# Hybrid decoder trunk on one core: six places for split weights, earlier index scores, and a later scale and shift of the residual rows

## The chip, the cores and the metric

The kernel runs on 1 core of a Trainium2 chip. The metric is device microseconds (us) of one execution, and the median of several is compared. Engines are named as the profile names them: PE (TensorE matmuls), PEld (TensorE weight loads), DVE (VectorE), ACT (ScalarE), POOL (GpSimd) and SP (SyncE, which issues most DMAs).

## The reference

One decoder layer on 512 tokens of width 1024, everything in float32. Each of three sub-layers is applied as h <- LayerNorm(ALPHA * h + f(h)).

1. Token mixing. One input projection feeds three groups of heads: gated linear attention (GLA, 4 heads), sparse attention (DSA, 5 heads) and stick-breaking attention (SB, 5 heads). The outputs are concatenated and go through `w_out`.
2. Cross-attention with 4 heads into 256 memory tokens (`w_mem_q`, `w_mem_kv`, `w_mem_o`).
3. A squared-ReLU MLP of hidden width 4096 (`w_up`, `w_down`).

The sparse attention picks its keys by an index score:

```python
rel = relu(einsum('bthd,bsd->bths', iq, ik))         # 8 index heads of 64
isc = einsum('bths,bth->bts', rel, iw) * idx_scale   # weighted sum over the heads
isc = where(causal, isc, -inf)
_, idx = top_k(isc, 128)                             # keys that query t may see
```

## The kernel before

All matmuls of projections take fp32r operands in two parts, a rounded high part and the rest. A weight tile of 128x1024 is loaded by a DMA into one of 4 places (`wr_pool`), `split` (L419) writes the high part to one of 5 places in `wh_pool` and the low part to one of 5 in `wl_pool` (L383, L384), and `mm3` (L414) makes three matmuls of each pair. Other tiles lie in 31 pages of 4 KB per partition (`page`, L392), 8 half-size places of 2 KB (`temp`, L395), 8 PSUM banks, and in constants of their own (`cst`). The constants `scan_mask`, `rel`, `cmask_f`, `cmask`, `tri_f`, `ones_f` and `w2p` are such.

The stages come in this order: LayerNorm of the input and its transposes; the index projection `ik` and four tiles `iq` of two heads each; GLA value, query and key projections (`gv_glr`, three `gqk_tile`, L674); index scores and top-k; GLA; SB; DSA with the keys and values of the memory between; `w_out` with a norm (`after_mix`, L1147); the four memory heads; `w_mem_o` with a norm (`after_mem`, L1198); the MLP, whose up part interleaves with seven-product down part (`first_products`, L1271; `second_parts`, L1319).

A matmul group that gets `split=True` (L590) makes its 512 columns in two halves of 256, so that it can start when only the first half of the tokens is normed. Of the `iq` tiles, heads 0, 2 and 4 are split so.

For each block j = 1 to 3 of 128 queries the index scores take eight heads of two matmuls, a Relu on ACT and a multiply-add on DVE into `acc` (128 x 128(j+1)). `top_k(j)` (L712) then makes 16 rounds of `max` and `match_replace` on DVE, and at the end writes the mask `E[j]`, which only DSA reads (L1038).

**What sets the order.** No instruction is issued when the Python code reaches it. `Program.either` (L163) records it with a priority, the running counter `nc.clock`, which grows by one per instruction. At the end `Program.issue` (L240) lays all of them out by a list scheduler: each engine takes the ready instruction that can start first, and among equals the one with the lowest priority number; an instruction is only looked at when its number is at most `LOOK` = 560 ahead of the first one not yet issued, and a tile is only handed out early when its pool has a place left for all that comes before it (`slots`, L275). Each engine then runs its list in that order. So a change of a priority or of a pool's size can reorder every engine's list.

A piece of code can move its instructions in that order by changing the counter. Top-k does so, one round every `TOPK_STRETCH` = 10 instructions:

```python
start = nc.clock
for n, _ in enumerate(s for j in range(1, NT) for s in top_k(j)):
    nc.clock = start + (n + 1) * TOPK_STRETCH
nc.clock = start
```

and so does the scale and shift of the residual rows, which are normed in place (`center`, L518) and whose gain and bias are needed only when the row is next added to:

```python
def gain_shift(hat, gb, t, later=0.0):
    nc.clock += later
    any_tt(hat[t], hat[t], gb[0], OP.mult)
    any_tt(hat[t], hat[t], gb[1], OP.add)
    nc.clock -= later
```

`any_tt` (L407) offers an instruction to DVE first and to POOL second. Behind `w_out` and behind `w_mem_o` four rows of 128x1024 each get a multiplication and an addition, `GAIN_LATER` = 400 instructions behind (L1155, L1209); their rows of gain and bias take two pages till then.

Of the kernel before, what the change touches and what calls it, by code (L numbers as in the profile page):

```python
# [364 lines left out]
def trunk_kernel(ctx: ExitStack, tc: tile.TileContext, x, mem, ln_in_g, ln_in_b, w_in, gate_w2,  # L365
# [17 lines left out]
    wh_pool = pool("wh", "wh", 5)  # L383
    wl_pool = pool("wl", "wl", 5)  # L384
# [58 lines left out]
    scan_mask = cst.tile([128, 512], F32, "scan_mask")  # L443
# [125 lines left out]
    rel = cst.tile([128, 512], F32, "rel")  # L569
    nc.gpsimd.iota(rel, pattern=[[1, 512]], base=-384, channel_multiplier=-1, allow_small_or_imprecise_dtypes=True)  # L570
    cmask_f = cst.tile([128, 128], F32, "cmask_f")
    nc.gpsimd.memset(cmask_f, 1.0)
    nc.gpsimd.affine_select(out=cmask_f, in_=cmask_f, pattern=[[1, 128]], compare_op=OP.is_ge, fill=0.0,
                            base=0, channel_multiplier=-1)
    nc.gpsimd.memset(cmask_f[0:64, 64:128], 0.0)
    cmask = cst.tile([128, 128], U32, "cmask")
    nc.vector.tensor_copy(cmask, cmask_f)
    tri_f = cst.tile([128, 128], F32, "tri_f")
# [5 lines left out]
    ones_f = cst.tile([128, 128], F32, "ones_f")  # L584
# [106 lines left out]
    E_pg = [page([1024], F32, "E012"), page([512], F32, "E3")]  # L691
    E = [E_pg[0][:, 0:128], E_pg[0][:, 128:384], E_pg[0][:, 384:768], E_pg[1][:, 0:512]]
    accs = {}
    for j in range(1, NT):
        n = 128 * (j + 1)
        acc = temp(f"acc{j}")
        accs[j] = acc
        for h in range(IDX_H):
            ps = bank("ps_idx")
            for i in range(2):  # L700
                mm(ps[:, :n], iq[h][:, 128 * j:128 * j + 128], ik[:, i, 0:n], i == 0, i == 1)
            r = temp("r")
            nc.scalar.activation(r[:, :n], ps[:, :n], AF.Relu)
            if h == 0:
                nc.vector.tensor_scalar(acc[:, :n], r[:, :n], iw[:, j, 0:1], None, op0=OP.mult)
            else:
                nc.vector.scalar_tensor_tensor(acc[:, :n], r[:, :n], iw[:, j, h:h + 1], acc[:, :n],
                                               op0=OP.mult, op1=OP.add)
        nc.gpsimd.affine_select(out=acc[:, n - 128:n], in_=acc[:, n - 128:n], pattern=[[-1, 128]],
                                compare_op=OP.is_ge, fill=MASKED, base=0, channel_multiplier=1)  # L710

    def top_k(j):  # L712

        n = 128 * (j + 1)
        acc = accs[j]
        for _ in range(TOPK // 8):
            m8 = tiny(8, "m8")
            nc.vector.max(m8, acc[:, :n])
            nc.vector.match_replace(out=acc[:, :n], in_to_replace=m8, in_values=acc[:, :n], imm_value=TAKEN)
            yield  # L720
# [11 lines left out]
    w2p = cst.tile([16, 2, 2, 64], F32, "w2p")  # L732
# [34 lines left out]
    for i in range(1, 3):  # L767
        gqk_tile(i)
# [648 lines left out]
```

## Time and profile before

| what | value |
|---|---|
| median of 3 runs | 826.19 us (826.02 to 827.07) |
| the profiled execution | 825.4 us, of which the span from the first to the last instruction is 823.6 us |
| PE busy | 792.5 us (96% of the span), 4177 matmuls |
| PEld busy | 662.8 us (80%) |
| DVE busy | 631.3 us (77%) |
| ACT busy | 329.2 us (40%) |
| POOL busy | 158.2 us (19%) |
| DMA | 106.70 MB, mean 130 GB/s |

Busy time is the union of an engine's instructions. A matmul's end is modelled, so a busy PE can still be short of its best pace; start times of neighbouring matmuls show the pace. An idle stretch of an engine is put down to the instruction that released it last. Times in the rows count from the span's start.

### The profile page before, as it was taken

The numbers are of one execution on the slowest core, as the hardware profiler recorded it, in microseconds if no ns is written. First come the engines' busy times: TensorE is split into PE (matmuls) and PEld (weight loads), VectorE is DVE, ScalarE is ACT, GpSimd is POOL, SyncE is SP. The second block draws the span as 40 slices with busy tenths as digits, with TensorE's granted clock in tenths as the row PEclk, the third lists the DMA queues.
The fourth block names the chain that finished last, engine by engine and source line by source line (L and its number), as shares of the span: only waits on it lengthen the run. The fifth ranks groups of instructions, "written<-read, shape, count | busy, mean of one in ns | idle before, by whom it ended". The sixth has DMA issues, their size and how long they took to land.

```text
span 823.6 us, 11289 instructions
## 1 busy us (share of the span) xinstructions
PE 792.5 (96%) x4177; PEld 662.8 (80%) x4177; DVE 631.3 (77%) x1111; ACT 329.2 (40%) x634; POOL 158.2 (19%) x173
## 2 busy tenths in 40 slices
PE   7999999999999899989999989999999999899995
PEld 5997769777877888888878889888888888678884
DVE  7737999997649983886553799767777776798778
ACT  4506634577535540233330143333323232585420
POOL 5320142354622210227340210000000000110001
PEclk9999999999999999999999999999999999999998
DMA  8520331603244534023322024645546555467532
GB/s 239 137 53 15 100 94 27 179 9 103 75 152 159 165 120 150 27 77 103 114 92 77 26 77 142 217 154 186 197 137 214 196 174 175 138 219 240 196 126 103
DMA packets 99927, 106.70 MB, mean 130 GB/s; under 512 B 10448, under 2 KB 79136, under 8 KB 99872
## 3 DMA queue, kind: packets, MB, share of 16 engines
q1 hardware_dynamic: 97344, 99.00, 38.1%
q10 hardware_dynamic: 2528, 6.98, 2.5%
q8 instruction: 33, 0.54, 0.3%
q14 instruction: 22, 0.18, 0.1%
HBM read 94.69 MB, written 10.49 MB: 128 GB/s over the span
## 4 chain that ended last, share of the span: by engine, by line
PE 68%; DVE 16%; issue 2%; ACT 1%; DMA 1%; POOL 0%; DVEq 0%; ACTq 0%; POOLq 0%
PE ps_up L356 20%; PE ps_dn L356 17%; PE ps_wmo L356 4%; PE ps_wo L356 4%; PE ps_q L356 3%; DVE res L356 2%; PE ps_km L356 2%; PE ps_z L356 2%; DVE acc L356 2%; PE ps_vm L356 2%; PE ps_gg L356 1%; PE ps_dq L356 1%; PE ps_mo L356 1%; DVE m L356 1%; DVE s L356 1%
## 5 line engine op out<-in xcount | busy, mean ns | idle before, releaser
L356 PE MATMUL ps_up<-h2T,h_up 128*128 128x512 f32 (+1 forms) x576 | 161.1, 366 | 0.0
L356 PEld LDWEIGHTS ps_up<-h2T,h_up 128*128 128x128 f32 x576 | 104.0, 189 | 17.6 <-DVE h2T L356 0.2
L356 PE MATMUL ps_up<-h2T,l_up 128*128 128x512 f32 (+1 forms) x288 | 104.8, 366 | 0.5 <-DVE l_up L356 0.5
L356 ACT ACTIVATE ur<-ps_up,gb_all 128x512 f32<-128x512 f32 x32 | 22.1, 690 | 108.7 <-PE ps_up L356 108.7
L356 PEld LDWEIGHTS ps_up<-h2T,l_up 128*128 128x128 f32 x288 | 54.1, 189 | 9.5 <-DVE l_up L356 0.7
L356 PE MATMUL ps_dn<-h_dn,a 128*128 128x512 f32 x192 | 59.3, 389 | 0.0
L356 DVE TENSOR_TENSOR l_dn<-r_dn,h_dn 128x1024 fp32r<-128x1024 f32 (+1 forms) x44 | 45.2, 1026 | 5.1 <-ACT h_dn L356 3.7
L356 PE MATMUL ps_dn<-h_dn,ends 128*128 128x512 f32 x128 | 47.7, 396 | 0.7 <-DVE ends L356 0.7
L356 POOL TENSOR_TENSOR a<-keep,a 128x1024 fp32r<-128x1024 f32 x1 | 4.1, 4067 | 228.3 <-PE ps_dn L356 228.3
L356 PE MATMUL ps_q<-h1T,h_wmq 128*128 128x256 f32 (+1 forms) x192 | 45.7, 329 | 0.0
L356 ACT ACTIVATE h<-ps_lt,gb_all 128x256 f32<-128x256 f32 x20 | 10.2, 566 | 85.6 <-PE ps_lt L356 84.8
L356 PEld LDWEIGHTS ps_dn<-h_dn,a 128*128 128x128 f32 x192 | 36.0, 188 | 7.5
L356 PE MATMUL ps_wmo<-h_wmo,oT 128*128 128x512 f32 x128 | 40.7, 393 | 0.0
L356 DVE TENSOR_TENSOR l_up<-r_up,h_up 128x1024 fp32r<-128x1024 f32 x32 | 38.9, 1220 | 2.2 <-ACT h_up L356 0.5
L356 PE MATMUL ps_wo<-h_wo,mix 128*128 128x512 f32 x128 | 40.3, 392 | 0.0
L356 PE MATMUL ps_dn<-l_dn,a 128*128 128x512 f32 x96 | 37.3, 389 | 0.0
L356 PEld LDWEIGHTS ps_q<-h1T,h_wmq 128*128 128x128 f32 x192 | 32.9, 197 | 2.5 <-DVE h1T L356 0.2
L356 PE MATMUL ps_q<-h1T,l_wmq 128*128 128x256 f32 (+1 forms) x96 | 31.3, 330 | 0.5 <-DVE ve_mix L356 0.5
L356 DVE TENSOR_SCALAR h_up<-r_up 128x1024 fp32r<-128x1024 f32 x17 | 11.8, 692 | 26.1 <-PE ps_up L356 22.6
L356 PEld LDWEIGHTS ps_dn<-h_dn,ends 128*128 128x128 f32 x128 | 24.5, 192 | 6.3 <-DVE ends L356 1.2
L356 PEld LDWEIGHTS ps_wo<-h_wo,mix 128*128 128x128 f32 x128 | 24.0, 188 | 4.9
L356 PEld LDWEIGHTS ps_wmo<-h_wmo,oT 128*128 128x128 f32 x128 | 24.0, 188 | 4.8
(408 smaller groups left out, 2095.6 us busy)
## 6 DMA issues: line engine op xcount, KB each, us to landing
r_dn<-in_w_down_dram SPq DMA_DIRECT2D x48, 512.0 KB, 4.3
r_up<-in_w_up_dram SPq DMA_DIRECT2D x32, 512.0 KB, 4.5
r_t<-t SPq DMA_DIRECT2D x16, 512.0 KB, 3.6
r_kvv<-in_w_mem_kv_dram SPq DMA_DIRECT2D x8, 512.0 KB, 4.0
r_kvk<-in_w_mem_kv_dram SPq DMA_DIRECT2D x8, 512.0 KB, 3.6
r_wo<-in_w_out_dram SPq DMA_DIRECT2D x8, 512.0 KB, 4.4
r_wmq<-in_w_mem_q_dram SPq DMA_DIRECT2D x8, 512.0 KB, 5.0
r_wmo<-in_w_mem_o_dram SPq DMA_DIRECT2D x8, 512.0 KB, 3.4
```

The costliest lines, as they stand in the source:

```text
L356: f(*[real(a) for a in args], **{k: real(a) for k, a in kwargs.items()})
```

## The change

It does three things.

First, `wh_pool` and `wl_pool` get 6 places each instead of 5. The room comes from the constants: `scan_mask` and `rel` share one page (`masks`), and `cmask_f`, `cmask`, `tri_f`, `ones_f` and `w2p` become half-size places that are handed on when their last reader is done. `cmask` is made just ahead of GLA. In `first_weights` the order in which the two pairs of places are asked for changes, not their number.

Second, the index scores of a pair of heads are recorded right behind the `iq` tile of the next pair, and those of the last pair at the head of `top_k(j)`; top-k starts right behind the last tile, ahead of `gv_glr`, one round every 18 instructions instead of 10. The third `iq` tile is no longer split in halves. The first `gqk_tile`, which was recorded ahead of the index scores, now follows with the other two behind the decay terms.

Third, `GAIN_LATER` is 900 instead of 400.

```diff
-    wh_pool = pool("wh", "wh", 5)
-    wl_pool = pool("wl", "wl", 5)
+    wh_pool = pool("wh", "wh", 6)
+    wl_pool = pool("wl", "wl", 6)
...
-    scan_mask = cst.tile([128, 512], F32, "scan_mask")
+    masks = page([2, 512], F32, "masks")
+    scan_mask, rel = masks[:, 0, :], masks[:, 1, :]
...
-    rel = cst.tile([128, 512], F32, "rel")
...
-    tri_f = cst.tile([128, 128], F32, "tri_f")
+    tri_f = temp("tri_f", 128)
...
-    ones_f = cst.tile([128, 128], F32, "ones_f")
+    ones_f = temp("ones_f", 128)
...
-    iq = new_q("iq", IDX_H)
-    for h in range(0, IDX_H, 2):
-        ps = proj_T([(C_IQ + 64 * h, 128, 0)], "iq", split=h < 6, weights=second if h == 0 else None)
-        for e in range(2):
-            stack(iq[h + e], ps, 64 * e, 1.0)
...
+    iq = new_q("iq", IDX_H)
+    accs = {j: temp(f"acc{j}") for j in range(1, NT)}
+
+    def index_scores(h, j):
+
+        n, acc = 128 * (j + 1), accs[j]
+        ps = bank("ps_idx")
+        for i in range(2):
+            mm(ps[:, :n], iq[h][:, 128 * j:128 * j + 128], ik[:, i, 0:n], i == 0, i == 1)
+        r = temp("r")
+        nc.scalar.activation(r[:, :n], ps[:, :n], AF.Relu)
+        if h == 0:
+            nc.vector.tensor_scalar(acc[:, :n], r[:, :n], iw[:, j, 0:1], None, op0=OP.mult)
+        else:
+            nc.vector.scalar_tensor_tensor(acc[:, :n], r[:, :n], iw[:, j, h:h + 1], acc[:, :n],
+                                           op0=OP.mult, op1=OP.add)
+
+    def iq_tile(h):
+        ps = proj_T([(C_IQ + 64 * h, 128, 0)], "iq", split=h < 4, weights=second if h == 0 else None)
+        for e in range(2):
+            stack(iq[h + e], ps, 64 * e, 1.0)
+
+    for h in range(0, IDX_H, 2):
+        iq_tile(h)
+        if h:
+            for j in range(1, NT):
+                for e in range(2):
+                    index_scores(h - 2 + e, j)
...
+        for e in range(2):
+            index_scores(IDX_H - 2 + e, j)
+        nc.gpsimd.affine_select(out=acc[:, n - 128:n], in_=acc[:, n - 128:n], pattern=[[-1, 128]],
+                                compare_op=OP.is_ge, fill=MASKED, base=0, channel_multiplier=1)
...
-    start, nc.pace = nc.clock, GQK_PACE
-    gqk_tile(0)
-    nc.clock, nc.pace = start, 1.0
...
-    w2p = cst.tile([16, 2, 2, 64], F32, "w2p")
+    w2p = temp("w2p", 256)[0:16].reshape(2, 2, 64)
...
+    cmask_f = temp("cmask_f", 128)
...
+    cmask = temp("cmask", 128, U32)
+    nc.vector.tensor_copy(cmask, cmask_f)
...
-    for i in range(1, 3):
+    for i in range(3):
         gqk_tile(i)
...
-        hi = [wh_pool.tile([128, n], F32R, f"h_dn{n}") for n in (512, 1024)]
-        lo = [wl_pool.tile([128, n], F32R, f"l_dn{n}") for n in (512, 1024)]
+        left = [wh_pool.tile([128, 512], F32R, "h_dnl"), wl_pool.tile([128, 512], F32R, "l_dnl")]
+        hi, lo = wh_pool.tile([128, 1024], F32R, "h_dn"), wl_pool.tile([128, 1024], F32R, "l_dn")
...
-TOPK_STRETCH = 10.0
+TOPK_STRETCH = 18.0
...
-GAIN_LATER = 400.0
+GAIN_LATER = 900.0
```

## Rows read from the trace of the kernel before

**Rows 1.** The page: span and busy time of the engines.
```profile
span 823.6 us, 11289 instructions
PE 792.5 (96%) x4177; PEld 662.8 (80%) x4177; DVE 631.3 (77%) x1111; ACT 329.2 (40%) x634; POOL 158.2 (19%) x173
```

**Rows 2.** Windows: stretch, length, busy us of PE, PEld, DVE, ACT, POOL; PEclk; DMA.
```profile
40.00:64.00 24.00, 24.00 (x133) 22.57 (x132) 8.87 (x12) 4.47 (x14) 5.97 (x5) 1.00 0.22 60
...
85.00:187.00 102.00, 98.53 (x532) 77.40 (x532) 99.75 (x231) 53.61 (x135) 35.90 (x44) 1.00 0.30 82
...
222.00:305.00 83.00, 79.96 (x536) 67.19 (x535) 67.18 (x144) 40.45 (x96) 22.70 (x16) 1.00 0.46 150
...
350.00:362.00 12.00, 9.59 (x65) 9.14 (x64) 10.96 (x17) 1.14 (x2) 2.93 (x2) 0.86 0.32 92
...
385.00:465.00 80.00, 78.77 (x405) 66.61 (x404) 40.30 (x82) 17.74 (x49) 19.71 (x12) 1.00 0.28 87
...
476.00:488.00 12.00, 9.65 (x80) 9.17 (x78) 11.26 (x19) 2.42 (x5) 2.92 (x2) 1.00 0.35 104
...
490.00:704.00 214.00, 214.00 (x999) 179.60 (x999) 159.59 (x245) 68.79 (x105) 0.00 (x0) 1.00 0.53 174
704.00:724.00 20.00, 16.57 (x64) 12.70 (x62) 19.38 (x32) 12.20 (x18) 4.07 (x1) 0.91 0.52 172
```

**Rows 3.** Waits of PE: what waited <- for whom: us in total, times, longest.
```profile
PE ps_lt L356 <- DVE mv_mix L356: 1.9, 1, 1.9
...
PE ps_lt L356 <- DVE mv_mem L356: 1.9, 1, 1.9
PE ps_mpt L356 <- DVE mp L356: 1.7, 2, 1.2
...
PE ps_ms L356 <- DVE qT L356: 0.6, 1, 0.6
PE ps_q L356 <- DVE ve_mix L356: 0.5, 1, 0.5
PE ps_up L356 <- DVE l_up L356: 0.5, 1, 0.5
```

**Rows 4.** Timeline of DVE in the norm behind w_mem_o.
```profile
475.01 1.21 DVE L356 TENSOR_TENSOR res<-res,gbc_mem 128x1024 f32<-128x1024 f32 x1
...
478.71 1.22 DVE L356 TENSOR_TENSOR res<-res,bbc_mem 128x1024 f32<-128x1024 f32 x1
...
480.44 0.80 DVE L356 TENSOR_SCALAR res<-res,mv_mem,rs_mem 128x1024 f32<-128x1024 f32 x1
```

**Rows 5.** Timeline of POOL in the same norm: the reciprocal root of two rows.
```profile
459.75 0.55 POOL L356 TENSOR_TENSOR rs_mem<-ve_mem,mhalf 128x1 f32<-128x1 f32 x1 [32.29 <-DVE ve_mem L356]
...
478.87 1.46 POOL L356 TENSOR_TENSOR rs_mem<-ve_mem,mhalf 128x1 f32<-128x1 f32 x1 [6.68 <-DVE ve_mem L356]
```

**Rows 6.** Timeline of PE behind the stall in the mix norm.
```profile
357.81 0.64 PE L356 MATMUL ps_q<-h1T,h_wmq 128*128 128x256 f32 x2
358.24 0.42 PE L356 MATMUL ps_q<-h1T,l_wmq 128*128 128x256 f32 x1
358.45 0.63 PE L356 MATMUL ps_q<-h1T,h_wmq 128*128 128x256 f32 x2
```

**Rows 7.** Lines of DVE in 40:180, index work: busy us, mean ns, idle before.
```profile
L356 DVE MATCH_REPLACE8 acc<-m,acc 128x256 f32<-128x256 f32 (+2 forms) x48 | 25.9, 542 | 0.1
L356 DVE MAX8 m<-acc 128x8 f32<-128x256 f32 (+2 forms) x48 | 25.9, 550 | 0.3
L356 DVE SCALAR_TENSOR_TENSOR acc<-r,iw,acc 128x256 f32<-128x256 f32 (+2 forms) x21 | 12.8, 609 | 2.8 <-ACT r L356 2.4
```

**Rows 8.** Timeline of PE at the step from a split iq tile to the unsplit one.
```profile
38.88 0.40 PE L356 MATMUL ps_iq<-h0T,h_iq 128*128 128x256 f32 x2
...
39.24 0.63 PE L356 MATMUL ps_iq<-h0T,h_iq 128*128 128x512 f32 x2
...
44.48 0.39 PE L356 MATMUL ps_iq<-h0T,l_iq 128*128 128x512 f32 x1
```

More of the change, by code (lines that the diff above doesn't have):

```diff
@@ L566, in trunk_kernel @@
             ln_transposed(x_pg, *gb_cols["in"], hT, t - 1, 2)
-    rel = cst.tile([128, 512], F32, "rel")
     nc.gpsimd.iota(rel, pattern=[[1, 512]], base=-384, channel_multiplier=-1, allow_small_or_imprecise_dtypes=True)
[L571 to L577, printed above, removed]
-    tri_f = cst.tile([128, 128], F32, "tri_f")
+    tri_f = temp("tri_f", 128)
     nc.gpsimd.memset(tri_f, -1.0)
@@ L658, in trunk_kernel, with top_k @@
     nc.scalar.copy(iw, ps)
+    iq = new_q("iq", IDX_H)
[22 more added lines that the diff above has]
+                    index_scores(h - 2 + e, j)
+    E_pg = [page([1024], F32, "E012"), page([512], F32, "E3")]
+    E = [E_pg[0][:, 0:128], E_pg[0][:, 128:384], E_pg[0][:, 384:768], E_pg[1][:, 0:512]]
+    def top_k(j):
+        n = 128 * (j + 1)
+        acc = accs[j]
+        for e in range(2):
+            index_scores(IDX_H - 2 + e, j)
+        nc.gpsimd.affine_select(out=acc[:, n - 128:n], in_=acc[:, n - 128:n], pattern=[[-1, 128]],
+                                compare_op=OP.is_ge, fill=MASKED, base=0, channel_multiplier=1)
+        for _ in range(TOPK // 8):
+            m8 = tiny(8, "m8")
+            nc.vector.max(m8, acc[:, :n])
+            nc.vector.match_replace(out=acc[:, :n], in_to_replace=m8, in_values=acc[:, :n], imm_value=TAKEN)
+            yield
+        msk = temp("msk", dtype=U32)
+        nc.vector.tensor_scalar(msk[:, :n], acc[:, :n], -2e38, None, op0=OP.is_lt)
+        nc.gpsimd.memset(E[j], MASKED)
+        nc.vector.copy_predicated(E[j], msk[:, :n], rel[:, 384 - 128 * j:512])
+        yield
+    start = nc.clock
+    for n, _ in enumerate(s for j in range(1, NT) for s in top_k(j)):
+        nc.clock = start + (n + 1) * TOPK_STRETCH
+    nc.clock = start
     gv = [page([2, 384], F32, f"gv{i}") for i in range(2)]
@@ L686, in gqk_tile @@
                 nc.sync.dma_start((gqT if n < GLA_H else gkT)[r:r + c1 - c0, p, :], raw[c0 - 128 * i:c1 - 128 * i])
-    start, nc.pace = nc.clock, GQK_PACE
-    gqk_tile(0)
-    nc.clock, nc.pace = start, 1.0
[L691 to L720, printed above, removed]
-        msk = temp("msk", dtype=U32)
-        nc.vector.tensor_scalar(msk[:, :n], acc[:, :n], -2e38, None, op0=OP.is_lt)
-        nc.gpsimd.memset(E[j], MASKED)
-        nc.vector.copy_predicated(E[j], msk[:, :n], rel[:, 384 - 128 * j:512])
-        yield
-    start = nc.clock
-    for n, _ in enumerate(s for j in range(1, NT) for s in top_k(j)):
-        nc.clock = start + (n + 1) * TOPK_STRETCH
-    nc.clock = start
-    w2p = cst.tile([16, 2, 2, 64], F32, "w2p")
+    w2p = temp("w2p", 256)[0:16].reshape(2, 2, 64)
     nc.gpsimd.memset(w2p, 0.0)
@@ L742, in trunk_kernel @@
     gb_cols["mix"], gb_cols["mem"] = gb_all[:2], gb_all[2:]
+    cmask_f = temp("cmask_f", 128)
+    nc.gpsimd.memset(cmask_f, 1.0)
+    nc.gpsimd.affine_select(out=cmask_f, in_=cmask_f, pattern=[[1, 128]], compare_op=OP.is_ge, fill=0.0,
+                            base=0, channel_multiplier=-1)
+    nc.gpsimd.memset(cmask_f[0:64, 64:128], 0.0)
+    cmask = temp("cmask", 128, U32)
+    nc.vector.tensor_copy(cmask, cmask_f)
     grow, ktT, keT = (page([2, T], F32, n) for n in ("grow", "ktT", "keT"))
@@ L1261, in first_weights @@
         any_tt(r1[:, L], r1[:, R], r1[:, L], OP.subtract)
-        hi = [wh_pool.tile([128, n], F32R, f"h_dn{n}") for n in (512, 1024)]
-        lo = [wl_pool.tile([128, n], F32R, f"l_dn{n}") for n in (512, 1024)]
-        split_weights(r0[:, L], hi[0], lo[0])
-        split_weights(r1, hi[1], lo[1])
-        return [(hi[0], lo[0]), (hi[1][:, R], lo[1][:, R]), (hi[1][:, L], lo[1][:, L])]
+        left = [wh_pool.tile([128, 512], F32R, "h_dnl"), wl_pool.tile([128, 512], F32R, "l_dnl")]
+        hi, lo = wh_pool.tile([128, 1024], F32R, "h_dn"), wl_pool.tile([128, 1024], F32R, "l_dn")
+        split_weights(r0[:, L], *left)
+        split_weights(r1, hi, lo)
+        return [left, (hi[:, R], lo[:, R]), (hi[:, L], lo[:, L])]
     banks = {}
```

## The prediction

> **What bounds the kernel now.** I read the page first: PE is busy for 792.5 of 823.6 us [rows 1], so it sets the time, and no change here removes much of its work. What can be won is PE's idle time and time at a lower clock. The windows then show where that lies [rows 2]: length less PE's busy time is 3.47 us in 85:187, 3.04 in 222:305, 2.41 in 350:362, 1.23 in 385:465, 2.35 in 476:488 and 3.43 in 704:724, while the 214 us of the MLP between have none. The rest of the idle time lies ahead of the first matmuls and behind the last, where the change does nothing. In four of these six stretches DVE is busy for over nine tenths of the time [rows 2], and in the waits of PE every large entry from the first norm to the MLP names DVE [rows 3]. So the question is whether DVE does the right thing first in those stretches.
>
> **Part 1, the scale and shift of the residual rows.** It removes nothing: eight instructions of 128x1024 behind each norm (four gains, four biases) move on by 500 numbers. In the norm behind w_mem_o two of them stand on DVE, 1.21 and 1.22 us, between the additions and the `center` at 480.44 that PE's transposes wait for [rows 4]. PE waits 1.9 us for that and 0.5 for the first low part behind it; the norm behind w_out has the same two waits, 1.9 and 0.5 [rows 3]. With 400 the scheduler may place these eight at once (it looks 560 ahead); with 900 only when 340 more instructions are out. So 1.21 + 1.22 = 2.43 us of DVE goes from ahead of waits of 2.4 us. I take 2.2 per norm, since `center` still waits for POOL's root: 4.4 us. Bounds: nothing, if other work fills the holes and is just as much in the way, and 4.8.
>
> The clock is a second term. Behind the stall in the mix norm the granted clock of 350:362 is 0.86 [rows 2]: three matmuls of 256 columns start 0.64 us apart there, from 357.81 to 358.45, at the lower of the two levels (1.2 GHz) [rows 6], against 0.36 us from 38.88 to 39.24 at 2.4 GHz [rows 8]. 0.14 of 12 us is 1.68 us of clock, hence 3.36 us at half of it; these matmuls would have taken 0.36/0.64 of that, so 1.5 us are lost. In 476:488 the clock stayed at 1.00 behind as long a wait [rows 2], so it does not fall each time, but without the stall I see no cause for it. I take 1.5; bounds 0 and 1.5.
>
> Later gains and biases stand among the softmax work of the first memory head, where PE waits 0.6 us for qT and 1.7 in two waits for mp [rows 3]. One of these two lies in 385:465, where PE idles 1.23 [rows 2]. I take 0.3 of a possible 1.1.
>
> Where do they go? Counted from the lines, the four memory heads are 178, 178, 130 and 130 instructions, and the residual addition of row 0 in w_mem_o follows some 770 behind the gains, ahead of number 900. It needs them, so they are late by their own number. But from about the second head on they may be placed, and an engine that would idle takes them: DVE idles 39.7 us in 385:465, POOL 60.3 [rows 2], for eight instructions of 1.2 us. Behind w_mem_o the next user is the end of the MLP, and DVE idles 54.4 us in 490:704 [rows 2]. Queued behind such a one on DVE can be a softmax step that PE waits for, so it can cost up to 1.2 us twice. I take 0.3; bounds 0 and 2.4. The two pages of gain and bias are held longer, in the heads where the pages have a few to spare.
>
> POOL's root takes 0.55 us in one row and 1.46 in the other, which starts 0.16 us behind DVE's bias addition [rows 5, 4]. The Trainium skill (GPSIMD Engine Reference, Key points) says that POOL shares its access to SBUF with VectorE when that runs an instruction with two SBUF inputs; these rows agree. By that rule the root too gets up to 0.9 us shorter per norm, but the moved instructions would slow POOL, or be slowed by it, where they land, so it speaks against counting their new place at nothing; the sum would not leave the bounds above, as the waits end at 2.4.
>
> **Part 2, early index scores and top-k.** The same 48 matmuls and the same DVE work, recorded earlier. The multiply-adds take 12.8 us and the rounds of top-k 25.9 + 25.9 [rows 7]. In 40:64 DVE is busy only 8.87 of 24 us, so it has 15.1 us free just ahead of the stretch 85:187 in which it is busy 99.75 of 102 [rows 2]. The multiply-adds of heads 0 to 5 fit there and ahead of it, with some rounds for j = 1, so the full stretch gets lighter by 15 us or more, and top-k at 18 numbers a round yields to GLA and SB. No one is kept waiting: E is read in DSA alone. What PE idles in 85:187 is 3.47 us. Part of that is the time that a chain takes and not a queue on DVE, so I take 1.5; bounds 0 and 3.5.
>
> On the other side, ACT does 18 Relus in the stretch of the `iq` tiles, and DVE the multiply-adds ahead of the splits of `gv_glr`; ACT is busy 4.47 of 24 us [rows 2], which hides it. The first `gqk_tile` moves past the loads of w2p, gate bias and column constants on SP's queue, with its weight load and its three small copies; its products are only read in GLA, and PE has other matmuls till then: nothing.
>
> The third `iq` tile, unsplit, has 24 matmuls of 512 columns instead of 48 of 256: 48 x 0.12 = 5.76 us (0.36 for three, as above) against 24 x 0.228 = 5.47 (from 39.24 to 44.48 in 23 steps): 0.3 us won [rows 8]. It comes when both halves are there.
>
> **Part 3, six places.** Splits may run one tile further ahead; 4 raw places still bound the loads. In the MLP PE does not idle [rows 2], so nothing there. At its end, 704:724, PE idles 3.43 us at a clock of 0.91, and in DSA 3.04 [rows 2]. A place more could let the last two weight pairs be split earlier, or reorder DVE to the worse. The trace shows no price: 0, between 4 us won and 3 lost. The price of the room is one page till DSA and one half-size place through GLA.
>
> **The sum.** 4.4 + 1.5 + 0.3 - 0.3 + 1.5 + 0.3 = 7.7 us, of which I take off 0.3 for what a new order of the front does to the first stages: 7.4. From the 825.4 us of the profiled execution (the span of 823.6 and 1.8 around it) this gives 818.0; the median of the runs is 0.8 above that execution, so 818.8.
>
> **The rivals.** A, only the norms pay: DVE stays full through 85:187 because freed time is filled with splits, and the chains of GLA and SB are what PE waits for. For it: PE is busy 98.53 of 102 us although DVE has no free time [rows 2], so DVE's queue costs little there. 826.2 - 4.4 = 821.8, and 823 if the clock falls as before and a moved gain meets the softmax.
>
> B, slower: the half-size places run short. Through GLA two accumulators, cmask, three gates and the squares hold 7 of 8, where cmask had its own room; through the first SB heads the last accumulator stays, as its last round now has a number some 250 later. Then SB's chain cannot start ahead and PE has nothing to fill in. The price of a wait of that kind is 1.7/2 = 0.85 us [rows 3]. Two for each of five SB heads and one for each of four GLA blocks make 14 x 0.85 = 11.9 us: 830.7. It decides from 11 such waits on (9.1 us: the sum and 1.7 for the bound). Against it: a list scheduler has 560 instructions to choose from, with projections among them. The Trainium skill (Perfetto Trace Analysis, Optimization Strategy) says that the same gap repeated on the engine that should be full can mean that buffers are short. PE's waits in GLA and SB before are few, so no run here shows it yet; after, it would be B's sign.
>
> C, no change: the norms get l_up and h1T splits in the place of the gains and the stalls stay as they are, so 825 to 826.
>
> D, all of it and the end of the MLP: six places also close 704:724 and half of DSA's idle time, 3.4 + 1.5 us more: 814.
>
> **How the numbers follow.** About 0.2% is what a measurement of this kernel can tell from no change (1.7 us). My forecast gets 0.48, A 0.22, D 0.06, C 0.11, B 0.13. Faster is the forecast, A and D: 0.76; the same is C, 0.11; slower is B, 0.13. The range goes from 813.5, D and the gains of part 3, to 826.0, where C begins to end; B and half of C are left out.
>
> **What would show it.** In the profile after: the waits of ps_lt for mv_mix and mv_mem gone or under 0.6 us, and no res<-res,gbc between `center` and the additions; PEclk near 1.00 in that stretch; multiply-adds of acc from about 30 us on and the last E well ahead of DSA; DVE below 99.75/102 in 85:187; gains and biases of the mix norm in the memory heads. I am wrong if the two norm stalls stay at 1.9 us, or if new waits of PE of 0.8 us and more repeat in 100:220.

## The result and the profile after

The changed kernel takes **830.99 us** (median of 5 runs, 829.51 to 832.49), the kernel before beside it 826.2 us (826.02 to 827.07): a ratio of 1.0054 [1.0039, 1.007]. It is slower by about 0.5%, where 818.8 us was forecast. The profiled execution took 830.99 us, with a span of 829.2.

The page after, against [rows 1]:

```profile
span 829.2 us, 11238 instructions
PE 799.0 (96%) x4153; PEld 666.2 (80%) x4153; DVE 640.5 (77%) x1118; ACT 327.9 (40%) x632; POOL 146.9 (18%) x168
```

PE has 24 matmuls fewer and is busy 6.5 us longer. The same stretches as [rows 2], shifted by what their stage moved (columns as there):

```profile
40.00:64.00 24.00, 23.92 (x126) 21.62 (x125) 19.23 (x40) 12.90 (x23) 6.13 (x5) 1.00 0.17 46
94.00:196.00 102.00, 98.34 (x512) 75.59 (x511) 85.76 (x183) 48.67 (x125) 32.38 (x45) 0.97 0.31 88
231.00:312.00 81.00, 80.86 (x533) 68.16 (x531) 66.99 (x150) 40.89 (x96) 16.70 (x14) 1.00 0.51 162
353.00:366.00 13.00, 12.63 (x101) 12.06 (x100) 10.28 (x24) 5.65 (x12) 1.89 (x4) 1.00 0.29 82
388.00:471.00 83.00, 78.27 (x384) 65.51 (x383) 53.98 (x90) 18.77 (x49) 21.36 (x13) 0.98 0.26 83
481.00:494.00 13.00, 10.59 (x85) 10.09 (x85) 9.93 (x18) 4.79 (x11) 5.02 (x5) 1.00 0.24 83
496.00:711.00 215.00, 215.00 (x1002) 180.34 (x1002) 164.64 (x248) 64.90 (x99) 0.00 (x0) 1.00 0.53 173
711.00:732.00 21.00, 17.65 (x68) 13.43 (x67) 20.83 (x35) 12.59 (x19) 4.00 (x1) 0.92 0.55 188
```

Read down the column of DVE first. 19.23 of 24 us instead of 8.87, then 85.76 of 102 instead of 99.75: the index work moved forward as the text of the change says, and the full stretch is 14 us lighter. Now the column of PE: it still idles 3.66 us in that stretch (3.47 before), and the clock is 0.97 instead of 1.00. DSA (231:312) lost its idle time, 0.14 us instead of 3.04. The mix norm (353:366) idles 0.37 instead of 2.41, at full clock. The norm behind w_mem_o (481:494) idles 2.41, as before. The memory heads (388:471) idle 4.73 us instead of 1.23, at a clock of 0.98 instead of 1.00. The starts of PE's matmuls show where the time goes: the change is 6.8 us behind at the last `ps_dq`, where DSA begins (222.3 us before, 229.1 now), only 4.3 at the last `ps_ol` of DSA (298.9 and 303.2), 1.1 ahead at the first `ps_ms` of the memory heads (370.2 and 369.1), and 5.8 behind at their last `ps_mo` (433.1 and 438.9); from there to the end little changes. So the front and the memory heads lose, DSA and the mix norm win. The waits of PE name these places:

```profile
PE ps_mpt L356 <- DVE mp L356: 3.8, 3, 1.9
...
PE ps_ms L356 <- DVE qT L356: 2.3, 2, 1.2
PE ps_ke L356 <- DVE keT L356: 2.2, 1, 2.2
PE ps_lt L356 <- DVE res L356: 2.1, 1, 2.1
...
PE ps_A L356 <- issue: 1.1, 1, 1.1
```

Against [rows 3], both norm stalls under their old names are gone, but one is back as `res`. The softmax waits (mp, qT) have grown from 2.3 to 6.1 us. Where GLA starts, the wait ahead of `ps_A` is new, and the wait for `keT` has grown from this one of the kernel before:

```profile
PE ps_ke L356 <- DVE keT L356: 1.1, 1, 1.1
```

Windows of 12 us show what follows those two:

```profile
88.00:100.00 12.00, 8.75 (x41) 6.93 (x40) 7.20 (x9) 3.80 (x7) 1.87 (x1) 1.00 0.72 215
100.00:112.00 12.00, 12.00 (x54) 8.57 (x54) 8.90 (x24) 5.15 (x18) 3.05 (x4) 0.72 0.49 115
112.00:124.00 12.00, 12.00 (x55) 7.22 (x55) 8.25 (x26) 2.95 (x16) 3.53 (x4) 1.00 0.18 45
```

PE idles 3.25 us in 88:100, and behind that the granted clock is 0.72 for 12 us: 3.4 us of clock lost.

### The profile page after: what moved, and what is told of

Its sections match the earlier page's. It is cut to its first block, busy times and chain, and to the rows that moved or that the text cites. A ratio compares the mean times of both kernels' runs of the same rounds, so it can differ in the third digit from the quotient of the medians.

```text
span 829.2 us, 11238 instructions
## 1 busy us (share of the span) xinstructions
PE 799.0 (96%) x4153; PEld 666.2 (80%) x4153; DVE 640.5 (77%) x1118; ACT 327.9 (40%) x632; POOL 146.9 (18%) x168
## 4 chain that ended last, share of the span: by engine, by line
PE 83%; DVE 9%; issue 2%; ACT 2%; DMA 1%; SPq 1%; POOL 1%; DVEq 0%; POOLq 0%; ACTq 0%
PE ps_up L356 20%; PE ps_dn L356 17%; PE ps_wmo L356 4%; PE ps_wo L356 4%; PE ps_vm L356 3%; PE ps_iq L356 3%; PE ps_q L356 3%; PE ps_z L356 3%; DVE res L356 2%; PE ps_gv_glr L356 2%; PE ps_gg L356 2%; PE ps_km L356 2%; PE ps_sv L356 2%; PE ps_sq L356 1%; PE ps_dq L356 1%
## 5 line engine op out<-in xcount | busy, mean ns | idle before, releaser
L356 DVE TENSOR_TENSOR l_dn<-r_dn,h_dn 128x1024 fp32r<-128x1024 f32 x28 | 34.2, 1222 | 3.0 <-ACT h_dn L356 1.7
L356 DVE TENSOR_SCALAR h_dn<-r_dn 128x1024 fp32r<-128x1024 f32 x14 | 9.7, 693 | 28.5 <-PE ps_up L356 28.1
L356 DVE MAX8 m<-acc 128x8 f32<-128x256 f32 (+2 forms) x48 | 26.8, 559 | 2.0 <-POOL acc L356 0.9
L356 PE MATMUL ps_dn<-h_dn,mid 128*128 128x512 f32 x64 | 25.5, 398 | 1.9 <-ACT mid L356 1.9
```

The lines of the kernel that those rows point to most:

```text
L356: f(*[real(a) for a in args], **{k: real(a) for k, a in kwargs.items()})
```

## The experiments

Beside each group of kernels the kernel before was run again (medians 825.5 to 826.2). The column PEclk is that of the window 76:160, GLA and the start of SB, in each run's own trace; 84 us times what is missing from 1.00 is the clock lost there, also while PE waits.

| run | us, median (lowest to highest, runs) | ratio [95%] | PEclk 76:160 |
|---|---|---|---|
| before_gain900 | 822.39 (820.89 to 822.61, 5) | 0.9953 [0.994, 0.9966] | 1.00 |
| gain400 | 834.03 (831.48 to 842.27, 6) | 1.012 [1.0082, 1.0158] | 1.00 |
| index_only | 823.82 (823.32 to 825.29, 6) | 0.9975 [0.9963, 0.9986] | 1.00 |
| index_late | 826.19 (823.01 to 831.59, 12) | 1.001 [0.9988, 1.0032] | 0.94 |
| gqk_five | 824.31 (822.85 to 829.83, 12) | 0.9989 [0.9975, 1.0003] | 1.00 |
| five | 828.25 (824.11 to 841.67, 12) | 1.0018 [1.0006, 1.003] | 0.96 |
| the change | 830.99 (829.51 to 832.49, 5) | 1.0054 [1.0039, 1.007] | 0.96 |
| gqk_ahead | 827.36 (824.86 to 829.95, 12) | 1.0017 [1.0005, 1.0029] | 1.00 |
| gqk_ahead_wmo | 824.13 (823.37 to 826.65, 11) | 0.9983 [0.9974, 0.9991] | 1.00 |
| bg900_wmo | 826.9 (826.54 to 828.14, 11) | 1.0013 [1.0004, 1.0021] | 1.00 |
| col_late | 847.15 (840.06 to 856.58, 6) | 1.0225 [1.0193, 1.0258] | 0.92 |
| six_only | 833.05 (832.36 to 833.82, 4) | 1.0084 [1.0071, 1.0097] | 0.92 |
| six_only_wmo | 832.92 (831.15 to 833.55, 5) | 1.0078 [1.0066, 1.009] | 0.90 |
| room_only | 831.61 (829.97 to 832.02, 5) | 1.0058 [1.0046, 1.007] | 0.90 |
| room_half10 | 839.34 (837.39 to 839.89, 4) | 1.0159 [1.0142, 1.0176] | 0.86 |
| room_start | 822.2 (821.31 to 822.57, 5) | 0.9954 [0.9939, 0.9969] | 1.00 |
| five_half10 | 825.21 (824.02 to 834.42, 12) | 1.0009 [0.9985, 1.0033] | 1.00 |
| **gqk_five_half10** | **819.47** (819.1 to 821.78, 6) | **0.9927 [0.9913, 0.9941]** | 1.00 |
| gqk_five_start | 824.42 (823.43 to 846.02, 11) | 0.9983 [0.9973, 0.9992] | not read |

PEclk is that of one execution, so where the lowest and the highest run of a kernel lie far apart it is a sample. Of gqk_five_start no row is used, since its profiled execution took 846.02 us, far from its median.

**The residual gains.** One line alone, on either kernel.

```diff
@@ gain400, against the change
-GAIN_LATER = 900.0
+GAIN_LATER = 400.0
@@ before_gain900, against before
-GAIN_LATER = 400.0
+GAIN_LATER = 900.0
```

> The changed kernel with GAIN_LATER at 400 again; all engine lists are the changed kernel's up to the norm behind w_out. Theory 1 (the moved gains and biases meet the softmax of the memory heads: by the spacing of the matmuls the memory heads lost 5.3 us and the norm behind w_out won 3.5): the time falls by about 2 us to 829, the stall of 1.9 us and a stretch at the lower clock come back in the norm, and the waits for mp and qT in the memory heads fall from 6.1 us to about 2.3. Rival (half-size places or weight places are what costs): the time stays at 831 within 0.8. Rival of the prediction (the later gains win 6 us): the time rises to 835 or more.

> The kernel before with GAIN_LATER at 900 and nothing else. Theory 1: the norm behind w_out wins 3.5 us, the norm behind w_mem_o next to nothing, the memory heads lose 4 to 5: 827 to 828, the same within what can be told or slower by 0.2%. The prediction's part 1: 820 to 822. Rival (the change's loss is all in the first 150 us): 826.2 within 0.8 or less.

Alone it wins 3.8 us, inside the change 3.0 (834.03 to 830.99). The mix norm gives it: in before_gain900 PE is busy 11.56 us there at a clock of 1.00, against 9.59 at 0.86 in [rows 2].

```profile
350.00:362.00 12.00, 11.56 (x95) 11.14 (x94) 9.83 (x20) 5.33 (x12) 1.45 (x4) 1.00 0.46 132
```

The norm behind w_mem_o gives nothing. No gain stands ahead of `center` there now, but `center` itself has grown (timelines of DVE and of POOL, changed kernel):

```profile
481.46 2.85 DVE L356 TENSOR_SCALAR res<-res,mv_mem,rs_mem 128x1024 f32<-128x1024 f32 x1 [0.67 <-POOL rs_mem L356]
```
```profile
480.87 0.55 POOL L356 TENSOR_TENSOR rs_mem<-ve_mem,mhalf 128x1 f32<-128x1 f32 x1 [5.30 <-DVE ve_mem L356]
481.39 2.37 POOL L356 TENSOR_TENSOR l_up<-r_up,h_up 128x1024 fp32r<-128x1024 f32 x1
```

0.80 us became 2.85 [rows 4] beside a split of `l_up` that POOL starts 0.07 us ahead of it; the 2.05 us more are about PE's wait of 2.1 for `res`. PE also asks for this row earlier: its transposes stand behind 6 matmuls of `ps_up`, where before 30 came first. before_gain900 has the same 2.85 and the same wait, and in its profiled execution the clock behind that is 0.92 in 465:478 and 0.94 in 478:490, some 1.8 us lost; index_only has the same wait with 1.00 in both. gain400's profile, too, shows that chance has a part: up to the norm behind `w_out` its engines have the same lists as the change, and PE idles 3.0 us in 88:100 as against 3.25, yet its clock is 1.00 in 100:112, where the change has 0.72. So a time of one execution may differ by 3.4 us there with nothing changed.

**The front: early index scores, memory moves, the late gqk tile.** First each part alone, on the kernel before with GAIN_LATER 900:

```diff
@@ index_only, against before_gain900 (the index part of the change's diff, whole)
-        ps = proj_T([(C_IQ + 64 * h, 128, 0)], "iq", split=h < 6, weights=second if h == 0 else None)
+        ps = proj_T([(C_IQ + 64 * h, 128, 0)], "iq", split=h < 4, weights=second if h == 0 else None)
...
+    def index_scores(h, j):
...
-TOPK_STRETCH = 10.0
+TOPK_STRETCH = 18.0
@@ index_late, against index_only
-    start, nc.pace = nc.clock, GQK_PACE
-    gqk_tile(0)
-    nc.clock, nc.pace = start, 1.0
...
-    for i in range(1, 3):
+    for i in range(3):
```

> The kernel before with GAIN_LATER 900 and the early index scores and top-k (with the third iq tile unsplit) alone: the first gqk tile ahead of w2p as before, constants and places as before. If early index scores are worth what the prediction gave them (1.8 us less): about 820.6, ps_z's waits near 2 us instead of 4.5, GLA's last ps_A near 120. Rival (they bring nothing, since PE in GLA and SB waits for chains, and the Relus and multiply-adds put the gv and gate work behind): 822.4 to 824, last ps_A at 121 us or later.

> Early index scores with constants and places as before (index_only, 823.82 us) and the three gqk tiles behind the gate work, as in the change. If the late gqk tile costs by itself: 827 or so, SP's gqT copies past 84 us instead of 77.6, keT at 97 us or later and the last ps_A near 128. If it costs only where half-size places are short: 824 within 1.

Early index scores alone cost 1.4 us. This is index_only in the very window of [rows 2]:

```profile
85.00:187.00 102.00, 100.28 (x532) 78.21 (x532) 84.66 (x181) 53.98 (x137) 28.87 (x40) 1.00 0.33 93
```

PE idles 1.72 us there instead of 3.47, about what was forecast. But it issues the same 532 matmuls in 102 us: what it idles less, it is busy longer. The last `ps_sv` starts at 146.8 us, in before_gain900 at 144.6, and the last `ps_dq` at 225.0 instead of 222.3. No single wait carries that, and from 40 us on the clock is 1.00 in both. Up to 222 us PE idles 2.5 us less than in before_gain900, so its matmuls take some 5 us more; by the spacing of their starts this is spread over many tiles, none of them over 1.2 us. What makes them longer is not shown.

With the gqk tiles last, the median is 2.4 us higher, and in the profiled execution the clock falls. The twelve runs of index_late lie in two groups: six took 823.0 to 824.9 us with a granted clock of 0.989 to 0.991 over the whole span, six took 827.5 to 831.6 with 0.977 to 0.983. The first group is as good as index_only, so, as far as these means tell, the late tile costs next to nothing here unless the clock falls.

Then the memory moves alone:

```diff
@@ room_only, against before_gain900
-    scan_mask = cst.tile([128, 512], F32, "scan_mask")
+    masks = page([2, 512], F32, "masks")
+    scan_mask, rel = masks[:, 0, :], masks[:, 1, :]
...
+    tri_f = temp("tri_f", 128)
+    ones_f = temp("ones_f", 128)
+    w2p = temp("w2p", 256)[0:16].reshape(2, 2, 64)
...
+    cmask_f = temp("cmask_f", 128)
...
+    cmask = temp("cmask", 128, U32)
@@ six_only, against room_only
-    wh_pool = pool("wh", "wh", 5)
-    wl_pool = pool("wl", "wl", 5)
+    wh_pool = pool("wh", "wh", 6)
+    wl_pool = pool("wl", "wl", 6)
@@ room_half10, against room_only
-    half = pool("half", "t2", 8)
+    half = pool("half", "t2", 10)
@@ room_start, against room_only (and cmask recorded where it was before)
-    w2p = temp("w2p", 256)[0:16].reshape(2, 2, 64)
-    cmask_f = temp("cmask_f", 128)
-    cmask = temp("cmask", 128, U32)
+    w2p = cst.tile([16, 2, 2, 64], F32, "w2p")
+    cmask_f = cst.tile([128, 128], F32, "cmask_f")
+    cmask = cst.tile([128, 128], U32, "cmask")
```

> The kernel before with 6 places for split weights, the room made as the change makes it, and GAIN_LATER 900; index scores, top-k and gqk tiles as before. Against before_gain900 it has the sixth places alone. Theory 3 (the sixth place wins about 3.5 us in DSA, where PE's waits for the softmax go, and loses about 5 in the memory heads, where splits of w_mem_o get among the softmax steps): 822.4 - 3.5 + 5 = 824. Rival (places cost nothing by themselves): 819. Rival B of the prediction (half-size places run short in GLA): GLA ends later than 127.6 by 4 us or more.

> The kernel before with GAIN_LATER 900 and, of the change, only the memory moves (masks page, tri_f, ones_f, w2p, cmask_f and cmask in half-size places, cmask recorded behind the column constants), five places. The same with six places took 833.05 us, and before with GAIN_LATER 900 alone 822.39. Theory 1 (the memory moves reorder the front: cmask, its fill and the freed constants now wait for half-size places, so GLA starts 11 us late): about 830, keT and the first ps_A as late as with six places (near 109 and 111 us), and ps_pt again at some 3 us of waits. Theory 2 (the sixth place lets DVE, ACT and POOL split weights ahead of GLA's chain, which puts it behind): about 823, the first ps_A near 100 us.

> The memory moves alone (room_only, 831.61 us) with ten half-size places for eight. If the moves act through the number of half-size places (r of the index scores, w2p and cmask in one pool): 822 to 825, the first ps_A back near 99 to 102 us instead of 112.2, no PE wait of 4 us for h_sv. If they act in another way (masks held in a page, another order of recording): 830 to 832 and the first ps_A at 110 us or later.

> The memory moves without cmask and w2p, which stay in their own room (five places, eight half-size places): the masks page and the two short-lived tri_f and ones_f are left of the moves, with the other names in the last weights' split. If cmask and w2p in half-size places are what cost 9.2 us: 822.4 within 1.5, the first ps_A near 99 us. If the masks page does (a page less until DSA): 828 or more, the first ps_A late.

six_only was the surprise, and room_only shows that the sixth place isn't its reason: the moves alone cost 9.2 us, and all of that goes with `cmask` and `w2p` (their room, and the later place at which `cmask` is recorded), as room_start stands at 822.2. The windows of room_only, room_half10 and room_start, in this order:

```profile
88.00:100.00 12.00, 12.00 (x52) 9.11 (x51) 11.97 (x36) 3.97 (x9) 1.06 (x2) 1.00 0.01 2
100.00:112.00 12.00, 7.80 (x35) 6.29 (x33) 9.80 (x22) 7.63 (x15) 3.03 (x3) 0.85 0.55 170
112.00:124.00 12.00, 12.00 (x67) 8.75 (x67) 8.80 (x29) 4.13 (x23) 6.85 (x6) 0.72 0.46 117
```
```profile
100.00:112.00 12.00, 8.70 (x37) 6.48 (x37) 9.31 (x24) 4.43 (x10) 8.91 (x5) 0.59 0.54 142
112.00:124.00 12.00, 12.00 (x31) 6.64 (x31) 6.40 (x20) 1.12 (x9) 3.31 (x3) 0.50 0.09 24
```
```profile
100.00:112.00 12.00, 12.00 (x63) 7.88 (x62) 11.50 (x38) 5.46 (x20) 9.10 (x7) 1.00 0.62 165
112.00:124.00 12.00, 11.80 (x81) 8.72 (x81) 11.56 (x35) 5.78 (x27) 3.70 (x5) 1.00 0.17 44
```

In 76:160 the lost clock is 0.10 x 84 = 8.4 us in room_only and 0.14 x 84 = 11.8 in room_half10, of the 9.2 and 16.9 us that they take longer than before_gain900. PE also idles 3.9 and 2.3 us more there than in before_gain900, and part of the lost clock falls on these waits, so the shares can't simply be added; but the clock is the larger term in both. The chain in room_only, by the timelines of PE, ACT, SP and PE again:

```profile
80.45 3.08 PE L356 MATMUL ps_u<-glrT,w2p 16*128 16x512 f32 x4 [1.55 <-ACT r L356]
```
```profile
95.97 0.21 ACT L356 COPY gb_all<-ps_c 128x64 f32<-128x64 f32 x1 [8.43 <-PE ps_c L356]
```
```profile
100.28 1.16 SPq L356 DMA_DIRECT2D gqT<-gqk  x2
```
```profile
109.88 0.63 PE L356 MATMUL ps_sv<-h_sv,h0T 128*128 128x320 f32 x1 [4.20 <-ACT h_sv L356]
```

PE waits 1.55 us for a Relu ahead of `ps_u`. ACT stands 8.43 us at the copy of `gb_all` with the second gate's work and the gqk copies behind it; so SP can issue the small copies to `gqT` only at 100.28 (86.20 in before_gain900), the loads of `r_gg` and `r_sv` behind them on the same queue come late, and PE waits 4.2 us for `h_sv`. That the moved tiles run the half-size places short is not shown: ten places make it worse, not better, which neither theory had expected. What is shown is that the moves of these two tiles change the engines' lists, and where that ends; whether the pool or the later recording of `cmask` does it, no run separates. Why the lists come out so, stays open.

Then the parts inside the change:

```diff
@@ gqk_ahead, against the change
+    start, nc.pace = nc.clock, GQK_PACE
+    gqk_tile(0)
+    nc.clock, nc.pace = start, 1.0
     w2p = temp("w2p", 256)[0:16].reshape(2, 2, 64)
...
-    for i in range(3):
+    for i in range(1, 3):
@@ col_late, against the change
-    *gb_all, bup = col_consts("gb_all", ln_mix_g[0], ln_mix_b[0], ln_mem_g[0], ln_mem_b[0], b_up[0])
...
     for i in range(3):
         gqk_tile(i)
+    *gb_all, bup = col_consts("gb_all", ln_mix_g[0], ln_mix_b[0], ln_mem_g[0], ln_mem_b[0], b_up[0])
```

> The changed kernel with the first gqk tile recorded ahead of the decay terms again, as before. Theory 2: its scatters leave SP's queue early, the loads of r_gg and r_sv behind them are in time, keT is ready earlier, PE's waits of 2.2 and 1.1 us at the head of GLA go and so does the stretch at the lower clock there: 825 to 828. Rival (half-size places or the interleaving of GLA's small matmuls with projections is what costs): 831 within 1.

> The changed kernel with the transposed column constants (gb_all) recorded behind the three gqk tiles instead of ahead of the decay terms. Theory 2a (ACT's list has the copy of gb_all ahead of the decay exponentials, and ACT idles 5.8 us for it, with the copies of the gqk tiles and SP's queue behind): the exponentials come 4 to 5 us earlier, keT is ready before PE needs it, the waits of 2.2 and 1.1 us at the head of GLA go: 825 to 828. Theory 2b (the three late scatters of the gqk tiles and the burst of weight loads behind them set keT): keT stays near 97 us and the time at 830 to 832.

gqk_ahead wins 3.6 us with six places; with five it is 3.9 (five against gqk_five). In the change, SP's queue stands still from 50.65 us until the gqk copies are made (timelines of SP and ACT):

```profile
84.81 3.12 SPq L356 DMA_DIRECT2D gqT<-gqk  x5
88.03 1.86 SPq L356 DMA_DIRECT2D gkT<-gqk  x2
89.99 1.15 SPq L356 DMA_DIRECT2D r_gg<-in_w_in_dram  x2
91.23 1.05 SPq L356 DMA_DIRECT2D r_sv<-in_w_in_dram  x1
92.37 1.79 SPq L356 DMA_DIRECT2D gkT<-gqk  x3
```
```profile
81.83 0.21 ACT L356 COPY gb_all<-ps_c 128x64 f32<-128x64 f32 x1 [5.76 <-PE ps_c L356]
```

In before_gain900 three of the ten copies were out by 73 us; here all come together with the loads. But that is not what gqk_ahead takes away (its timeline of SP, and its window 88:100):

```profile
49.13 8.37 SPq L356 DMA_DIRECT2D r_gg<-in_w_in_dram  x2
...
84.08 3.87 SPq L356 DMA_DIRECT2D gqT<-gqk  x5
...
93.01 1.79 SPq L356 DMA_DIRECT2D gkT<-gqk  x3
```
```profile
88.00:100.00 12.00, 10.99 (x56) 8.53 (x55) 9.03 (x12) 6.21 (x13) 1.53 (x2) 1.00 0.74 212
```

The ten copies leave together there too, and the last of them even later than in the change (93.01 us, 92.37). So the path that was expected, copies that leave early, did not occur, and the queue of copies isn't the reason. What differs is that a second load of `r_gg` is out by 57.5 us, ahead of the halt, where the change has one until 89.99; that PE gets 56 matmuls out in 88:100 instead of 41, waits 1.0 us for `keT` instead of 2.2 and nothing at `ps_A`; and that the clock stays at 1.00. five and gqk_five differ in the same way. No run moves that load alone, so it isn't shown to be the cause.

The copy of `gb_all` looked like the cause as well, as ACT stands 5.76 us at it ahead of the gate's exponentials. col_late takes it out of the way and is slower by 16 us, the profiled execution, one of its fastest, by 10: GLA runs at a clock of 0.80 and 0.64 in 100:124. So that theory falls.

**The sixth place.** five takes it back in the change; five_half10 uses its room for two more half-size places. The names with wmo hold loads and splits of w_mem_o to numbers at most 150 ahead. gqk_five_start is gqk_five_half10 with `w2p`, `cmask_f` and `cmask` in `cst`, by the same lines as room_start.

```diff
@@ five, against the change; gqk_five, against gqk_ahead
-    wh_pool = pool("wh", "wh", 6)
-    wl_pool = pool("wl", "wl", 6)
+    wh_pool = pool("wh", "wh", 5)
+    wl_pool = pool("wl", "wl", 5)
@@ five_half10, against five; gqk_five_half10, against gqk_five
-    half = pool("half", "t2", 8)
+    half = pool("half", "t2", 10)
@@ six_only_wmo, gqk_ahead_wmo and bg900_wmo (before_gain900), each against its namesake
+            nc.ahead = ahead
             wh, wl = load_rows(w, 128 * (k0 + k), name)
+            nc.ahead = 1e9
...
-    gemm_tok(oT, w_mem_o, 0, NK, "wmo", after_mem)
+    gemm_tok(oT, w_mem_o, 0, NK, "wmo", after_mem, ahead=WMO_AHEAD)
...
+WMO_AHEAD = 150.0
```

> The changed kernel with 5 places for split weights again, the constants left where the change put them. Theory 2 (the loss of the front comes from the late gqk tile and from what stands in the lists ahead of the decay products, not from places): 831 within 2 us, and GLA still ends some 8 us later than before. Rival (the sixth place lets splits of weights that are not there yet stand ahead of the decay products on DVE): the splits of h_gg and h_sv move behind keT and the time falls to 826 or 827.

> The same with the loads and splits of w_mem_o allowed only 150 instructions ahead, so that they cannot get among the softmax of the memory heads. Theory 3: PE's waits for mp and qT in the memory heads are 2.4 us or less in sum, DSA keeps its 3.5: 818 to 820, less than both kernels. Rival (the heads' waits come from the moved gains and biases): as six_only, within 1 us.

> The changed kernel with the first gqk tile ahead again, as gqk_ahead, and the same limit on w_mem_o. Theory 3: 827.4 less the 5 us of the memory heads, 822 to 823. Rival (the limit does not reach what is in the way): 827 within 1. Beside six_only_wmo it shows what early index scores are worth: if they pay, it is the faster of the two by 2 us or more; if SB's gain only pays for GLA's loss, it is slower by 2 to 4.

> The kernel before with GAIN_LATER 900 (822.39 us) and the loads and splits of w_mem_o held to 150 numbers ahead. With six places the same limit won 3.2 us, where splits of w_mem_o stood among the heads' softmax. If that is the sixth place's own fault: no change with five, 822.4 within 0.8, ps_mpt's waits as before (1.5). If splits of w_mem_o meet the softmax with five places too: about 821, ps_mpt under 1 us.

The sixth place costs 2.7 us (828.25 to 830.99), and 3.05 with the gqk tile ahead. It wins in DSA, where five keeps PE's 3.0 us of waits. It loses more in the memory heads: from the first `ps_ms` to the last `ps_mo` they take 62.6 us in five, as before (62.9), and 69.8 in the change. Most of that is in the third head (DVE, then POOL):

```profile
402.06 2.35 DVE L356 TENSOR_TENSOR res<-res,gbc_mix 128x1024 f32<-128x1024 f32 x2
404.32 4.05 DVE L356 TENSOR_TENSOR res<-res,bbc_mix 128x1024 f32<-128x1024 f32 x2
...
408.90 2.79 DVE L356 TENSOR_TENSOR l_wmo<-r_wmo,h_wmo 128x1024 fp32r<-128x1024 f32 x1
...
414.11 2.00 DVE L356 TENSOR_SCALAR mp<-mp,mst 128x256 f32<-128x256 f32 x1
```
```profile
407.39 3.21 POOL L356 TENSOR_TENSOR bbc_mem<-bbc_mem,bd 128x1024 f32<-128x1024 f32 x1
410.69 2.93 POOL L356 TENSOR_SCALAR h_wmo<-r_wmo 128x1024 fp32r<-128x1024 f32 x2
413.59 4.70 POOL L356 TENSOR_TENSOR l_wmo<-r_wmo,h_wmo 128x1024 fp32r<-128x1024 f32 x2
```

Splits of w_mem_o, which a sixth place allows earlier, and the moved gains stand among the softmax; a multiplication `mp` takes 2.00 us beside POOL's split, where most take 0.35. Of the two it is the splits that make the waits for `mp`. In gain400 no gain stands in this head, and PE waits as long (PE in the change, then in gain400):

```profile
416.15 0.44 PE L356 MATMUL ps_mpt<-ident,mp 128*128 128x128 f32 x2 [1.60 <-DVE mp L356]
418.50 1.12 PE L356 MATMUL ps_mpt<-ident,mp 128*128 128x128 f32 x4 [1.91 <-DVE mp L356]
```
```profile
415.48 0.44 PE L356 MATMUL ps_mpt<-ident,mp 128*128 128x128 f32 x2 [2.18 <-DVE mp L356]
417.83 1.11 PE L356 MATMUL ps_mpt<-ident,mp 128*128 128x128 f32 x4 [1.91 <-DVE mp L356]
```

All of gain400's waits for `mp` come to 6.6 us and its heads take 68.9 us, so its theory that the waits fall to about 2.3 failed. Only the waits for `qT`, 2.3 us in the change and none in gain400, go with the later gains.

The limit takes some of this back with six places (gqk_ahead_wmo, 827.36 to 824.13; from 385 us on the waits for mp go from 3.5 to 2.0 us, and those for qT of 1.2 are gone). In six_only_wmo they fall too, from 6.1 to 3.2 us in all, but the median does not follow (833.05 to 832.92, where 818 to 820 was expected). Nor is the limit a remedy by itself: with five places the same limit costs 4.5 us (822.39 to 826.9), as there it puts four waits of 4.7 us in all for mp into the heads, and the clock of 400:432 at 0.89.

> The changed kernel with five places (828.25 us) and two more half-size places (10 for 8), in the room that the sixth place took. Rival B of the prediction (half-size places run short through GLA and SB): 3 us or more less, some 824 to 825, GLA's last ps_A near 120 to 124 us instead of 128.3, and the SB heads' ps_z shorter. The rival theory (GLA is late because the gqk tiles and their small copies come last, not for room): 828 within 0.8, the last ps_A within 1 us of 128.3.

> The changed kernel with five places, ten half-size places and the first gqk tile ahead of w2p. If the three costs add (sixth place 2.7, half-size places 3.0, late gqk tile 3.6): 830.99 - 9.3 = 821.7, at or below before with GAIN_LATER 900 alone (822.4). If the half-size places and the late gqk tile are one cost seen twice (both make GLA's operands late): 824 to 825, as five_half10.

> gqk_five_half10 (819.47 us) with eight half-size places again: the changed kernel with five places and the first gqk tile ahead of w2p. The sixth place cost 2.7 us in the changed order, gqk_ahead stood at 827.36: if the costs add, 824.7, so that the two half-size places win 5. If the places matter only where GLA's operands come late: 820 to 821. In either case a granted clock of 1.00 from 76 to 160 us, as gqk_ahead had.

> gqk_five_half10 with cmask and w2p in their own room, so that two half-size places more are free through the gate work and GLA. If what counts is the number of free places: 819 or less, down to 818. If the order that the scheduler happens on is what counts, more than their number: anything from 819 to 826, and above 822 as soon as the granted clock of 76 to 160 us falls under 1.00.

Two more half-size places win 3.0 us with the gqk tile late and 4.8 with it ahead, more than if the costs added (821.7 was expected). gqk_five_half10, at 819.47, beats the kernel before by 0.7% and the change by 1.4%. Its front has hardly any idle time and no fallen clock, and more matmuls are out in each window than in the change:

```profile
88.00:100.00 12.00, 12.00 (x69) 10.08 (x68) 9.25 (x17) 8.34 (x18) 1.84 (x2) 1.00 0.60 179
100.00:112.00 12.00, 11.97 (x68) 7.97 (x68) 11.29 (x30) 5.28 (x26) 4.75 (x6) 1.00 0.64 159
112.00:124.00 12.00, 12.00 (x67) 7.91 (x68) 9.64 (x28) 4.31 (x18) 3.27 (x3) 1.00 0.08 16
```

But gqk_five_start, with still more room in that pool, is 5 us slower again. So it isn't the count of places that decides; that it is the list which the scheduler happens on is what is left, and no run shows which difference of the lists does it.

## Why the prediction was wrong

Single steps lead from one kernel to the other: before 826.2; gains later 822.39 (-3.8); early index scores 823.82 (+1.4, index_only); memory moves 824.31 (+0.5, gqk_five); the gqk tiles last 828.25 (+3.9, five); the sixth place 830.99 (+2.7). The moves' +0.5 holds in this order alone; without early index scores they cost 9.2. From the 7.4 us that were to be won to the 4.8 that were lost is 12.2 us: the largest piece is the first gqk tile, taken at nothing, then part 2, the sixth place and part 1.

- **Part 1** was right in mechanism for one of the two norms: 3.8 us for some 5.9. The mix norm paid its stall and its clock: from the last `ps_wo` to the first `ps_ms` it is 20.4 us before and 16.4 in before_gain900, 4.0 won for 2.2 + 1.5. The term that failed is the second norm's 2.2: the stall is 2.1 us there as before, since POOL's split of `l_up` came beside `center`, which went from 0.80 to 2.85 us. That is what the bound "nothing, if other work fills the holes" and rival C had named. The text did name the rule of the Trainium skill (GPSIMD Engine Reference, Key points) and kept it inside the bounds for the gains alone; the splits that move up beside `center` were not counted. The row agrees with that section also where it names a two-port mode of VectorE beside two SBUF inputs, since `center` has one tensor as input; that it ran in this mode no row shows.
- **Part 2**, "I take 1.5; bounds 0 and 3.5": the idle time did shrink by 1.75 us in index_only, but the stage ended later. The step that failed takes PE's idle time for the stage's loss; PE idled less and its matmuls took longer, for a reason that stays open. Rival A's argument that DVE's queue costs little there held, but not its premise that DVE stays full (84.66 of 102 us in index_only).
- "The first `gqk_tile` moves past the loads ... **nothing**" failed by 3.6 to 3.9 us, and by 2.4 in index_late. The step that failed is "PE has other matmuls till then": in the change PE gets 41 matmuls out in 88:100 where gqk_ahead has 56, waits 3.2 us for `keT` and at `ps_A`, and in the profiled execution loses 3.4 us of clock behind that. What holds PE up is not the tile's small copies, which leave as late in gqk_ahead; which instruction does, stays open.
- **Part 3**, 0 between 4 won and 3 lost: measured 2.7 lost, so inside its bounds. The wins in DSA were foreseen; the splits among the memory heads' softmax, 7.2 us between five and the change, were not. The moved gains, 0.3 with a "bound 2.4", cost some 0.9 in the heads (68.9 us in gain400, 69.8 in the change).
- **Not in the sum at all:** the granted clock in GLA. A clock term was taken for a stall that goes, none for one that comes; 0.72 in 100:112 is 3.4 us of the loss in the profiled execution.
- **Rival B** gave 830.7 us, but not by its mechanism: the waits of PE after 100 us and up to 220 hold one entry of 0.3 us, not eleven of 0.8. Half-size places matter in the changed order (3.0 and 4.8 us won; in five_half10 the last `ps_A` comes at 122.6 us instead of 128.3, as that theory expected), but room_half10 loses 7.7 with two more and gqk_five_start 5 with more room. So the premise that places run short is neither shown nor refuted, and the agreement of the numbers is chance.

## What to carry to other kernels

When a list scheduler lays out all engines, price each part of a change by a kernel that has that part alone: the parts here ran from -3.8 to +9.2 us, and one of them differed by 8.7 between two surroundings. When DVE is full and PE hardly waits, emptying DVE buys little. Ask of every step that feeds the start of a stage what PE still has to do until then, and which queue its loads and copies stand in; and add the clock that PE may lose if it then waits.

## What the runs showed of the hardware

- The clock can cost more than the wait ahead of it: in room_half10 PE waits 4.2 us in all around 100 us, for `keT` and at `ps_A`, and the clock is 0.59, 0.50 and 0.92 in the three windows of 12 us from 100 on, some 12 us lost, although the profile shows PE busy for 12.00 of 12 us in 112:124 (31 matmuls, where room_start has 81).
- The idle time alone doesn't tell whether it falls: PE idles 5.93 us in 76:160 in five_half10 at a clock of 1.00, and 3.28 in the change at 0.96.
- The same lists may get either clock: 0.72 in the change, 1.00 in gain400, same window. In index_late the runs of one kernel differ by 8.6 us, with 0.991 to 0.977 over the span.
- POOL and DVE slow each other: `center` 0.80 to 2.85 us, `mp` 0.35 to 2.00, two bias additions 4.05 for 2 x 1.22 in [rows 4]; on POOL a reciprocal root 0.55 to 1.46 [rows 5], and the addition to `bbc_mem` 3.21 in the change for 2.39 in gain400.
